# Global average pooling over rows of 8192: loads of 8 MB and 16 MB in turn, and rows summed as two halves

## The chip, the core and the metric

The kernel runs on one core of a Trainium2 chip. The time is that of one execution on the device in microseconds (us); each kernel has the median of several runs. The profile shows one further execution, whose length is its span, from the first instruction to the last.

The engines that matter are VectorE (DVE in the profile) and ScalarE (ACT), which do the sums, SyncE (SP), which only waits and issues transfers, and the 16 DMA engines, which bring the data from HBM into SBUF. TensorE is not used, and GpSimd (POOL) sets four constants at the start.

## The reference

```
x: (64, 256, 8192) float32
reference(x) = mean of x over its last axis      # (64, 256) float32
```

These are 16384 rows of 8192 numbers, 536.87 MB, read once; 65.5 KB are written. Each number takes part in one addition.

## The kernel before, in words

**How the rows are laid out.** The 16384 rows are seen as one long list. Each of the 128 partitions has 128 rows, in two parts: `own`, R = 111 rows that follow each other in memory, and `own2`, R2 = 17 rows from the end of the list. With L = 8192, a row is 32 KB on a partition. One row of `own` (its first) and one of `own2` (its last) are kept for the end; the other 126 rows per partition come in pairs, 63 loads of [128, 2L], 8 MB each.

**The buffers.** There are three, `bufs[0]` to `bufs[2]`, of 64 KB per partition each. Each has a semaphore that tells that its load has landed (`in_sems`) and one that counts how often it was read out (`free_sems`).

**SyncE** issues every transfer, in the order in which they stand (lines 97 to 129). The first load is cut into 1 MB and 7 MB (line 99), loads two and three follow at once (line 103). Then a loop (line 109) and a written-out rest (line 116) go around the buffers: wait until VectorE and ScalarE have both read the buffer, then issue its next load. After the last pair comes the tail: one row per partition, 4 MB, into the first half of `bufs[0]` (line 120), and the other one in six pieces of falling size (line 123), five into the second half of `bufs[0]` and the last into `fin`. At the end SyncE waits for VectorE twice and stores the results of `own` and `own2` (lines 125 and 127).

**VectorE** waits for a load and sums the first row of the pair into a column of `res` (line 136, a reduction). **ScalarE** waits for the same load, scales the second row by 1/L in place, and its accumulator gives the mean, written straight to the output tile `outsb` (line 174). So each load is read by both at the same time, and its buffer is free when the slower one is done.

**The tail.** VectorE first scales all of its sums into `outsb` (line 148). Then it takes 15/32 of the 4 MB row (line 156) while ScalarE takes the rest (line 186), and `total` (line 142) adds the two parts and scales. The pieces of the last row are split in the same way (lines 161 and 189). The last piece, in `fin`, has the partial sums beside it, and one more `total` adds and scales it all. Its store ends the kernel.

Of the kernel before, what the change touches and what calls it, by code (L numbers as in the profile page):

```python
# [6 lines left out]
ADD = mybir.AluOpType.add  # L7
MULT = mybir.AluOpType.mult
X = mybir.AxisListType.X
COPY = mybir.ActivationFunctionType.Copy  # L10


def bass_global_avg_pool_1d_kernel(
    nc: bass.Bass,
    x: bass.AP,
    out: bass.AP,
):
    P = 128
    B, C, L = x.shape
    rows = B * C  # L20
    assert rows % (2 * P) == 0 and L % 64 == 0
    inv = 1.0 / float(L)

    R2 = 17
    R = rows // P - R2
    assert R % 2 == 1 and R2 % 2 == 1
    NBUF = 3  # L30
    N1, N2 = R // 2, R2 // 2
    NFULL = N1 + N2
    NLOOP = NFULL // NBUF
    NLOAD = N1 // NBUF
    assert NLOOP * NBUF == NFULL and NLOAD >= 2
    M = P * R

    flat = x.rearrange("b c l -> (b c) l")
    own = flat[0:M, :].rearrange("(p r) l -> p (r l)", p=P)
    own2 = flat[M:rows, :].rearrange("(p r) l -> p (r l)", p=P)  # L40
    out_flat = out.rearrange("b c -> (b c)")
    out_own = out_flat[0:M].rearrange("(p r) -> p r", p=P)
    out_own2 = out_flat[M:rows].rearrange("(p r) -> p r", p=P)

    ch = [L // 2, 17 * L // 64, 7 * L // 64, L // 16, 3 * L // 128, 5 * L // 128]
    dve = [53 * L // 256, 13 * L // 128, 17 * L // 256, 5 * L // 256, 3 * L // 128]
    assert sum(ch) == L
    NCH = len(ch)  # L50
    NS = NCH - 2
    offs = [sum(ch[:c]) for c in range(NCH)]
    NPART = 2 * NS + 1

    with ExitStack() as ctx:
        sb = lambda n, s: ctx.enter_context(nc.sbuf_tensor(n, s, F32))
        sem = lambda n: ctx.enter_context(nc.semaphore(n))

        sb("pad0", [P, 32])

        fin = sb("fin", [P, 384])
        scaled = sb("scaled", [P, 384])
        half = sb("half", [P, 32])
        scaled_half = sb("scaled_half", [P, 32])
        res = sb("res", [P, 64])
        outsb = sb("outsb", [P, R + R2])
        sb("pad1", [P, 960])
        bufs = [sb(f"buf{i}", [P, 2 * L]) for i in range(NBUF)]

        in_sems = [sem(f"in_sem{i}") for i in range(NBUF)]  # L70
        free_sems = [sem(f"free_sem{i}") for i in range(NBUF)]
        tile_sem = sem("tile_sem")
        ch_sems = [sem(f"ch_sem{i}") for i in range(NCH)]
        act_sem = sem("act_sem")
        dve_sem = sem("dve_sem")
        out_sems = [sem(f"out_sem{i}") for i in range(2)]

        tail = bufs[0]
        D = 15 * L // 32

        def chunk(c):
            if c == NCH - 1:
                return fin[:, 0 : ch[c]]
            return tail[:, L + offs[c] : L + offs[c] + ch[c]]

        part = lambda i: fin[:, ch[-1] + i : ch[-1] + i + 1]

        D_HALF, D_TILE = 2, 3  # L90
        D_PART = D_TILE + NS + 1
        D_LAST = D_PART + 1

        A_HALF, A_PART = 1, 1 + NS


        eng = nc.sync
        for a, w in ((0, L // 4), (L // 4, 2 * L - L // 4)):
            eng.dma_start(bufs[0][:, a : a + w], own[:, L + a : L + a + w]).then_inc(  # L99
                in_sems[0], 16  # L100
            )
        for b in range(1, NBUF):
            eng.dma_start(bufs[b][:], own[:, (2 * b + 1) * L : (2 * b + 3) * L]).then_inc(
                in_sems[b], 16
            )
        with eng.Fori(1, NLOAD) as i:
            for b in range(NBUF):
                eng.wait_ge(free_sems[b], i * 2)
                eng.dma_start(  # L109
                    bufs[b][:], own[:, bass.ds((i * NBUF + b) * (2 * L) + L, 2 * L)]  # L110
                ).then_inc(in_sems[b], 16)
        for g in range(NLOAD * NBUF, NFULL):
            b = g % NBUF
            eng.wait_ge(free_sems[b], g // NBUF * 2)
            of, a = (own, 2 * g + 1) if g < N1 else (own2, 2 * (g - N1))
            eng.dma_start(bufs[b][:], of[:, a * L : (a + 2) * L]).then_inc(
                in_sems[b], 16
            )
        eng.wait_ge(free_sems[0], 2 * NLOOP)
        eng.dma_start(tail[:, 0:L], own[:, 0:L]).then_inc(tile_sem, 16)  # L120
        for c in range(NCH):
            a = (R2 - 1) * L + offs[c]
            eng.dma_start(chunk(c), own2[:, a : a + ch[c]]).then_inc(ch_sems[c], 16)  # L123
        eng.wait_ge(dve_sem, D_TILE)
        eng.dma_start(out_own, outsb[:, 0:R]).then_inc(out_sems[0], 16)
        eng.wait_ge(dve_sem, D_LAST)
        eng.dma_start(out_own2, outsb[:, R : R + R2]).then_inc(out_sems[1], 16)
        for s in out_sems:
            eng.wait_ge(s, 16)


        eng = nc.vector
        with eng.Fori(0, NLOOP) as i:
            for b in range(NBUF):
                eng.wait_ge(in_sems[b], i * 16 + (16 if b else 32))
                eng.tensor_reduce(  # L136
                    res[:, bass.ds(i * NBUF + b, 1)], bufs[b][:, 0:L], X, ADD
                ).then_inc(free_sems[b], 1)

        def total(to, junk, ap, after):  # L140
            eng.wait_ge(dve_sem, after)  # L141
            eng.tensor_scalar(  # L142
                junk, ap, inv, None, MULT, ADD, accum_out=to
            ).then_inc(dve_sem, 1)

        for b in range(NBUF):
            eng.wait_ge(free_sems[b], 2 * NLOOP)
        eng.tensor_scalar(  # L148
            outsb[:, 1 : 1 + 2 * NFULL].rearrange("p (n j) -> p j n", j=2)[:, 0],
            res[:, 0:NFULL],  # L150
            inv,
            None,
            MULT,
        ).then_inc(dve_sem, 1)
        eng.wait_ge(tile_sem, 16)
        eng.tensor_reduce(half[:, 0:1], tail[:, 0:D], X, ADD).then_inc(dve_sem, 1)  # L156
        eng.wait_ge(act_sem, A_HALF)
        total(outsb[:, 0:1], scaled_half[:, 0:2], half[:, 0:2], D_HALF)
        for c in range(NS + 1):
            eng.wait_ge(ch_sems[c], 16)  # L160
            eng.tensor_reduce(part(c), chunk(c)[:, 0 : dve[c]], X, ADD).then_inc(dve_sem, 1)  # L161
        eng.wait_ge(act_sem, A_PART)
        eng.wait_ge(ch_sems[NCH - 1], 16)
        w = ch[-1] + NPART
        total(outsb[:, 2 * NFULL + 1 : 2 * NFULL + 2], scaled[:, 0:w], fin[:, 0:w], D_PART)


        eng = nc.scalar
        eng.preload_act_table(COPY)  # L169
        with eng.Fori(0, NLOOP) as i:  # L170
            for b in range(NBUF):
                eng.wait_ge(in_sems[b], i * 16 + (16 if b else 32))
                ap = bufs[b][:, L : 2 * L]
                eng.activation(  # L174
                    ap,
                    ap,
                    COPY,
                    scale=inv,
                    accum_out=outsb[:, bass.ds((i * NBUF + b) * 2 + 2, 1)],
                ).then_inc(free_sems[b], 1)  # L180

        def summed(ap, to):
            eng.activation(ap, ap, COPY, accum_out=to).then_inc(act_sem, 1)  # L183

        eng.wait_ge(tile_sem, 16)
        summed(tail[:, D:L], half[:, 1:2])
        for c in range(NS):
            eng.wait_ge(ch_sems[c], 16)
            summed(chunk(c)[:, dve[c] :], part(NS + 1 + c))
# [28 lines left out]
```

## Time and profile before

| what | us |
|---|---|
| median of 3 runs (lowest, highest) | 1243.44 (1243.22, 1243.46) |
| span of the profiled execution | 1242.2 |
| VectorE busy | 556.4 |
| ScalarE busy | 458.6 |
| VectorE's waits for loads, before line 136 | 682.1 |
| ScalarE's waits for loads, before line 174 | 777.0 |
| SyncE's waits for VectorE at line 109, 51 of them | 964.1 |
| from issue to landing of an 8 MB load | 49.0 |

For the profiled execution the profile gives the span; the 1.2 us between it and the median lie outside its first and last instruction. A busy time is the sum of the engine's instructions; what is left of the span is waiting. A row of the groups gives line, engine, operation, output and input with their shapes, the count, then busy time and mean duration in ns, then the idle time just ahead of these instructions and what ended it. A row of the timeline starts with the start and the duration, both in us. A row of the chain is a step of the work that ended last, with start and duration; "SPq" and "DVEq" there are the engines' own waiting and issuing. "Landing" is the moment at which a transfer's semaphore says that all of it is there.

### The profile page before, as it was taken

Reading aid. Unit: us, or ns where it says so; the run is one execution under the profiler, and the core shown is the slowest. Engines: PE = TensorE matmul, PEld = TensorE weight load, DVE = VectorE, ACT = ScalarE, POOL = GpSimd, SP = SyncE. Lnnn points to the kernel's source line nnn. Section 1 sums busy time; section 2 is a strip of 40 time slices with the busy share of each in tenths; the row PEclk is TensorE's granted clock in tenths of the full one; section 3 lists DMA queues with packets and bytes.
Section 4 is the critical chain, followed back from the end, with each engine's and each line's share of the span. In section 5 each row is a group of like instructions: output and inputs, shape, how many; then the busy total and the mean of one; then the engine's idle time right before and its main releaser. Section 6 shows DMA issues by size and latency. Waiting matters only on the chain.

```text
span 1242.2 us, 756 instructions
## 1 busy us (share of the span) xinstructions
DVE 556.4 (45%) x74; ACT 458.6 (37%) x137; POOL 0.2 (0%) x4
## 2 busy tenths in 40 slices
DVE  2354353543534435345353453544535435354355
ACT  2243242442423424334243342433424324244245
POOL 0000000000000000000000000000000000000000
DMA  9999999999999999999999999999999999999998
GB/s 405 439 439 439 439 437 412 435 439 439 439 439 435 409 439 439 439 439 439 437 409 437 439 439 439 439 437 409 437 439 439 439 439 439 418 426 439 439 439 374
DMA packets 10512, 536.94 MB, mean 432 GB/s; under 512 B 1424, under 2 KB 1680, under 8 KB 1936
## 3 DMA queue, kind: packets, MB, share of 16 engines
q1 hardware_dynamic: 10512, 536.94, 99.8%
HBM read 536.87 MB, written 0.07 MB: 432 GB/s over the span
## 4 chain that ended last, share of the span: by engine, by line
DMA 84%; DVE 15%; SPq 0%; issue 0%; DVEq 0%
DMA buf<-in_x_dram 81%; DVE res L136 15%; DMA fin<-in_x_dram 4%; SPq L123 0%; SPq L109 0%; DVEq L136 0%; DVE scaled L142 0%; SPq L99 0%; SPq L120 0%; DVEq L141 0%
## 5 line engine op out<-in xcount | busy, mean ns | idle before, releaser
L136 DVE TENSOR_REDUCE res<-buf 128x8192 f32 x63 | 547.2, 8686 | 682.1 <-DMA buf<-in_x_dram 682.1
L174 ACT ACTIVATE buf<-buf 128x8192 f32<-128x8192 f32 x63 | 442.9, 7030 | 777.0 <-DMA buf<-in_x_dram 777.0
L174 ACT ACTIVATION_READ_ACCUMULATOR buf<-buf x63 | 11.7, 186 | 0.0
L183 ACT ACTIVATE buf<-buf 128x352 f32<-128x352 f32 (+3 forms) x5 | 8.3, 1663 | 3.6 <-DMA buf<-in_x_dram 3.6
L161 DVE TENSOR_REDUCE fin<-buf 128x1 f32<-128x1696 f32 (+4 forms) x5 | 4.2, 866 | 1.2 <-DMA buf<-in_x_dram 1.0
L156 DVE TENSOR_REDUCE half<-buf 128x1 f32<-128x3840 f32 x1 | 4.2, 4153 | 0.6 <-DMA buf<-in_x_dram 0.6
L169 ACT ACT_TABLE_LOAD x1 | 1.3, 1283 | 0.7 <-PEq L203 0.7
L183 ACT ACTIVATION_READ_ACCUMULATOR buf<-buf 128x1 f32 x5 | 0.9, 186 | 0.0
L142 DVE TENSOR_SCALAR_CACHE_REDUCE scaled<-fin 128x329 f32<-128x329 f32 x1 | 0.5, 497 | 0.2 <-DMA fin<-in_x_dram 0.2
L148 DVE TENSOR_SCALAR outsb<-res 128x63 f32<-128x63 f32 x1 | 0.2, 196 | 0.1
L142 DVE TENSOR_SCALAR_CACHE_REDUCE scaled_half<-half 128x2 f32<-128x2 f32 x1 | 0.2, 155 | 0.1
L203 POOL MEMSET const-bfloat16-1.0<- 128x1 bf16 x1 | 0.1, 101 | 0.0
L203 POOL MEMSET const-uint8-127<- 128x1 uint8 x1 | 0.1, 101 | 0.0
L203 POOL MEMSET const-float32-0.0<- 128x1 f32 x1 | 0.1, 98 | 0.2 <-issue 0.2
L203 POOL MEMSET const-float32-1.0<- 128x1 f32 x1 | 0.1, 98 | 0.0
L142 DVE DVE_READ_ACCUMULATOR scaled_half<-half 128x1 f32 x1 | 0.1, 83 | 0.0
L142 DVE DVE_READ_ACCUMULATOR scaled<-fin 128x1 f32 x1 | 0.1, 83 | 0.0
## 6 DMA issues: line engine op xcount, KB each, us to landing
buf<-in_x_dram SPq DMA_DIRECT2D x1, 7168.0 KB, 21.2
buf<-in_x_dram SPq DMA_DIRECT2D x1, 4096.0 KB, 39.5
buf<-in_x_dram SPq DMA_DIRECT2D x1, 2048.0 KB, 44.0
buf<-in_x_dram SPq DMA_DIRECT2D x1, 1088.0 KB, 46.1
buf<-in_x_dram SPq DMA_DIRECT2D x1, 1024.0 KB, 4.8
buf<-in_x_dram SPq DMA_DIRECT2D x62, 49.0
buf<-in_x_dram SPq DMA_DIRECT2D x1, 448.0 KB, 46.8
buf<-in_x_dram SPq DMA_DIRECT2D x1, 256.0 KB, 46.9
```

The source lines that it names most:

```text
L136: eng.tensor_reduce(res[:, bass.ds(i * NBUF + b, 1)], bufs[b][:, 0:L], X, ADD).then_inc(free_sems[b], 1)
L142: eng.tensor_scalar(junk, ap, inv, None, MULT, ADD, accum_out=to).then_inc(dve_sem, 1)
L148: eng.tensor_scalar(outsb[:, 1 : 1 + 2 * NFULL].rearrange("p (n j) -> p j n", j=2)[:, 0], res[:, 0:NFULL], inv, None, MULT,).then_inc(dve_ ...
L156: eng.tensor_reduce(half[:, 0:1], tail[:, 0:D], X, ADD).then_inc(dve_sem, 1)
L161: eng.tensor_reduce(part(c), chunk(c)[:, 0 : dve[c]], X, ADD).then_inc(dve_sem, 1)
L169: eng.preload_act_table(COPY)
L174: eng.activation(ap, ap, COPY, scale=inv, accum_out=outsb[:, bass.ds((i * NBUF + b) * 2 + 2, 1)],).then_inc(free_sems[b], 1)
L183: eng.activation(ap, ap, COPY, accum_out=to).then_inc(act_sem, 1)
L203: nc = _bacc.Bacc("TRN2", target_bir_lowering=False, num_devices=1)
```

## The change

- R2 goes from 17 to 19, and R from 111 to 109, so that both parts less one row are multiples of six.
- Three buffers of 64 KB per partition become two: `short` of 64 KB and `long` of 128 KB. A round loads two rows into `short` (8 MB) and the next four into `long` (16 MB). There are 21 rounds, 18 in `own` and 3 in `own2`: 42 loads in place of 63. SyncE waits for `short`, issues its load, waits for `long`, issues its load.
- In a round VectorE takes one row of `short` and three of `long`, ScalarE one of each.
- VectorE sums a row by a `scalar_tensor_tensor` of its two halves: the first half times 1.0 plus the second half, written over the first half, with the sum of the results in an accumulator. Before it was a reduction of the whole row.
- Before the tail VectorE scales its sums by two instructions, 21 x 1 and 21 x 3 columns, in place of one of 63 columns. They no longer count on `dve_sem`; the reduction of the half row counts two instead.
- The tail row and its pieces go to `short`. Their sizes, their split and their order stay.

```diff
-    R2 = 17
+    R2 = 19
     R = rows // P - R2
...
+    ROUND = 6
...
+    N1, N2 = (R - 1) // ROUND, (R2 - 1) // ROUND
+    NLOOP = N1 + N2
...
-        bufs = [sb(f"buf{i}", [P, 2 * L]) for i in range(NBUF)]
...
+        short = sb("short", [P, 2 * L])
+        long = sb("long", [P, 4 * L])
...
-        tail = bufs[0]
+        tail = short
...
+            eng.dma_start(short[:, a : a + w], own[:, L + a : L + a + w]).then_inc(in_s, 16)
+        eng.dma_start(long[:], own[:, 3 * L : 7 * L]).then_inc(in_l, 16)
+        with eng.Fori(1, N1) as i:
+            eng.wait_ge(free_s, i * 2)
+            eng.dma_start(short[:], own[:, bass.ds(i * (ROUND * L) + L, 2 * L)]).then_inc(in_s, 16)
+            eng.wait_ge(free_l, i * 4)
+            eng.dma_start(long[:], own[:, bass.ds(i * (ROUND * L) + 3 * L, 4 * L)]).then_inc(in_l, 16)
+        for g in range(N2):
...
+        eng.wait_ge(free_s, 2 * NLOOP)
         eng.dma_start(tail[:, 0:L], own[:, 0:L]).then_inc(tile_sem, 16)
...
+        def row(buf, r, to, free):
+            a = buf[:, r * L : r * L + L // 2]
+            b = buf[:, r * L + L // 2 : (r + 1) * L]
+            eng.scalar_tensor_tensor(a, a, 1.0, b, MULT, ADD, accum_out=to).then_inc(free, 1)
+
         with eng.Fori(0, NLOOP) as i:
-            for b in range(NBUF):
-                eng.wait_ge(in_sems[b], i * 16 + (16 if b else 32))
-                eng.tensor_reduce(
-                    res[:, bass.ds(i * NBUF + b, 1)], bufs[b][:, 0:L], X, ADD
-                ).then_inc(free_sems[b], 1)
+            eng.wait_ge(in_s, i * 16 + 32)
+            row(short, 0, res[:, bass.ds(i * 4, 1)], free_s)
+            eng.wait_ge(in_l, i * 16 + 16)
+            for r in range(3):
+                row(long, r, res[:, bass.ds(i * 4 + 1 + r, 1)], free_l)
...
+        eng.wait_ge(free_s, 2 * NLOOP)
+        eng.wait_ge(free_l, 4 * NLOOP)
+        rounds = outsb[:, 1 : 1 + ROUND * NLOOP].rearrange("p (n j) -> p n j", j=ROUND)
+        for to, of in ((0, 0), (2, 1)):
+            w = 3 if of else 1
+            eng.tensor_scalar(
...
         eng.wait_ge(tile_sem, 16)
-        eng.tensor_reduce(half[:, 0:1], tail[:, 0:D], X, ADD).then_inc(dve_sem, 1)
+        eng.tensor_reduce(half[:, 0:1], tail[:, 0:D], X, ADD).then_inc(dve_sem, 2)
...
+        def scaled_row(buf, r, to, free):
+            ap = buf[:, r * L : (r + 1) * L]
+            eng.activation(ap, ap, COPY, scale=inv, accum_out=to).then_inc(free, 1)
+
         with eng.Fori(0, NLOOP) as i:
...
+            eng.wait_ge(in_s, i * 16 + 32)
+            scaled_row(short, 1, outsb[:, bass.ds(i * ROUND + 2, 1)], free_s)
+            eng.wait_ge(in_l, i * 16 + 16)
+            scaled_row(long, 3, outsb[:, bass.ds(i * ROUND + 6, 1)], free_l)
```

More of the change, by code (lines that the diff above doesn't have):

```diff
@@ L22, in bass_global_avg_pool_1d_kernel @@
     inv = 1.0 / float(L)
-    R2 = 17
+    R2 = 19
     R = rows // P - R2
[L29 to L35, printed above, removed]
+    ROUND = 6
+    assert (R - 1) % ROUND == 0 and (R2 - 1) % ROUND == 0
+    N1, N2 = (R - 1) // ROUND, (R2 - 1) // ROUND
+    NLOOP = N1 + N2
     M = P * R
@@ L132, in bass_global_avg_pool_1d_kernel @@
         eng = nc.vector
+        def row(buf, r, to, free):
+            a = buf[:, r * L : r * L + L // 2]
+            b = buf[:, r * L + L // 2 : (r + 1) * L]
+            eng.scalar_tensor_tensor(a, a, 1.0, b, MULT, ADD, accum_out=to).then_inc(free, 1)
         with eng.Fori(0, NLOOP) as i:
-            for b in range(NBUF):
-                eng.wait_ge(in_sems[b], i * 16 + (16 if b else 32))
-                eng.tensor_reduce(
-                    res[:, bass.ds(i * NBUF + b, 1)], bufs[b][:, 0:L], X, ADD
-                ).then_inc(free_sems[b], 1)
+            eng.wait_ge(in_s, i * 16 + 32)
[3 more added lines that the diff above has]
+                row(long, r, res[:, bass.ds(i * 4 + 1 + r, 1)], free_l)
         def total(to, junk, ap, after):
@@ L144, in total @@
             ).then_inc(dve_sem, 1)
[L146 to L154, printed above, removed]
+        eng.wait_ge(free_s, 2 * NLOOP)
[4 more added lines that the diff above has]
+            eng.tensor_scalar(
+                rounds[:, :, to : to + w],
+                res[:, 0 : 4 * NLOOP].rearrange("p (n j) -> p n j", j=4)[:, :, of : of + w],
+                inv,
+                None,
+                MULT,
+            )
         eng.wait_ge(tile_sem, 16)
-        eng.tensor_reduce(half[:, 0:1], tail[:, 0:D], X, ADD).then_inc(dve_sem, 1)
+        eng.tensor_reduce(half[:, 0:1], tail[:, 0:D], X, ADD).then_inc(dve_sem, 2)
         eng.wait_ge(act_sem, A_HALF)
@@ L164, in bass_global_avg_pool_1d_kernel @@
         w = ch[-1] + NPART
-        total(outsb[:, 2 * NFULL + 1 : 2 * NFULL + 2], scaled[:, 0:w], fin[:, 0:w], D_PART)
+        total(outsb[:, R + R2 - 1 : R + R2], scaled[:, 0:w], fin[:, 0:w], D_PART)
         eng = nc.scalar
         eng.preload_act_table(COPY)
+        def scaled_row(buf, r, to, free):
+            ap = buf[:, r * L : (r + 1) * L]
+            eng.activation(ap, ap, COPY, scale=inv, accum_out=to).then_inc(free, 1)
         with eng.Fori(0, NLOOP) as i:
[L171 to L180, printed above, removed]
+            eng.wait_ge(in_s, i * 16 + 32)
+            scaled_row(short, 1, outsb[:, bass.ds(i * ROUND + 2, 1)], free_s)
+            eng.wait_ge(in_l, i * 16 + 16)
+            scaled_row(long, 3, outsb[:, bass.ds(i * ROUND + 6, 1)], free_l)
         def summed(ap, to):
```

33 lines of the change are left out of this document (9 added, 24 removed).

## The prediction

> **What bounds the kernel now.** I read the page first: the span, the 40 slices, the queues, the chain of work that ended last, the costliest groups.
>
> ```profile
> span 1242.2 us, 756 instructions
> ...
> DVE 556.4 (45%) x74; ACT 458.6 (37%) x137; POOL 0.2 (0%) x4
> ...
> GB/s 405 439 439 439 439 437 412 435 439 439 439 439 435 409 439 439 439 439 439 437 409 437 439 439 439 439 437 409 437 439 439 439 439 439 418 426 439 439 439 374
> DMA packets 10512, 536.94 MB, mean 432 GB/s; under 512 B 1424, under 2 KB 1680, under 8 KB 1936
> ...
> q1 hardware_dynamic: 10512, 536.94, 99.8%
> ...
> L136 DVE TENSOR_REDUCE res<-buf 128x8192 f32 x63 | 547.2, 8686 | 682.1 <-DMA buf<-in_x_dram 682.1
> L174 ACT ACTIVATE buf<-buf 128x8192 f32<-128x8192 f32 x63 | 442.9, 7030 | 777.0 <-DMA buf<-in_x_dram 777.0
> L174 ACT ACTIVATION_READ_ACCUMULATOR buf<-buf x63 | 11.7, 186 | 0.0
> ```
>
> The queue's packets fill 99.8% of the 16 DMA engines, while VectorE and ScalarE are idle for more than half the span and both wait for loads alone. So the stream of 536.94 MB sets the time, and faster arithmetic in the middle is worth nothing. Next the windows: the stretch between the first 8 MB landing and the last one, and the stretch in which the last 8 MB come in small pieces.
>
> ```profile
> 22.37:1220.47 1198.10, 538.53 (x62) 441.61 (x124) 0.00 (x0) 1.00 1.00 434
> 1220.47:1239.98 19.51, 17.38 (x10) 15.71 (x12) 0.00 (x0) 1.00 0.96 406
> ```
>
> The columns are length, VectorE, ScalarE and GpSimd busy, clock, DMA share, GB/s. In the stream the DMA share is 1.00. Whatever the change wins must come from outside VectorE and ScalarE there. What can still move is the end, and for it I read the timeline of VectorE.
>
> ```profile
> 22.52 8.69 DVE L136 TENSOR_REDUCE res<-buf 128x8192 f32 x1 [22.52 <-DMA buf<-in_x_dram]
> ...
> 1220.60 8.69 DVE L136 TENSOR_REDUCE res<-buf 128x8192 f32 x1 [10.68 <-DMA buf<-in_x_dram]
> 1229.42 0.20 DVE L148 TENSOR_SCALAR outsb<-res 128x63 f32<-128x63 f32 x1
> 1230.17 4.15 DVE L156 TENSOR_REDUCE half<-buf 128x1 f32<-128x3840 f32 x1 [0.55 <-DMA buf<-in_x_dram]
> 1234.46 0.15 DVE L142 TENSOR_SCALAR_CACHE_REDUCE scaled_half<-half 128x2 f32<-128x2 f32 x1
> 1234.55 0.08 DVE L142 DVE_READ_ACCUMULATOR scaled_half<-half 128x1 f32 x1
> 1234.99 1.92 DVE L161 TENSOR_REDUCE fin<-buf 128x1 f32<-128x1696 f32 x1 [0.36 <-DMA buf<-in_x_dram]
> 1237.59 2.38 DVE L161 TENSOR_REDUCE fin<-buf 128x1 f32<-128x832 f32 x4 [0.68 <-DMA buf<-in_x_dram]
> 1240.12 0.50 DVE L142 TENSOR_SCALAR_CACHE_REDUCE scaled<-fin 128x329 f32<-128x329 f32 x1 [0.15 <-DMA fin<-in_x_dram]
> 1240.54 0.08 DVE L142 DVE_READ_ACCUMULATOR scaled<-fin 128x1 f32 x1
> ```
>
> From the last big load on, VectorE waits four times for the next landing: 0.55, 0.36, 0.68 and 0.15 us. The first three, 1.59 us, are all the slack that it has behind the stream; work added there beyond 1.59 us moves the end.
>
> The median of the runs is 1243.44 us, 1.2 us above the profiled span; I add differences to the median.
>
> **The change part by part.**
>
> *63 loads become 42.* Row 1220.60 less row 22.52, over the 62 loads between, is 19.32 us per 8 MB load. What a load's boundary costs shows where the same bytes come in seven loads. The chain of waits gives the two landings:
>
> ```profile
> 22.52 8.70 DVE res L136
> 31.21 0.02 issue
> 31.23 0.07 SPq L109
> ...
> 31.40 49.00 DMA buf<-in_x_dram
> ...
> 1181.79 0.03 issue
> 1181.82 0.06 DVEq L136
> 1181.87 0.05 issue
> 1181.92 8.70 DVE res L136
> ...
> 1193.38 46.61 DMA fin<-in_x_dram
> 1239.98 0.02 issue
> ...
> 1240.12 0.50 DVE scaled L142 x2
> ```
>
> A landing stands 0.13 us ahead of the instruction that it releases (1181.79 to 1181.92). So the last big load landed at 1220.47, and the seven small ones were in at 1239.98: 19.51 us, 0.19 more than one load. Six further boundaries at 0.03 us each; 21 boundaries fewer are worth at most 21 x 0.03 = 0.7 us. The small loads also had seven packets where one load has one: the page's 10512 packets over 73 transfers (63 big loads, one of them in two parts; 7 small ones; 2 stores) are 144 each, 128 rows and 16 more. A 16 MB load has rows of 128 KB, and no row of that length is in this trace. If it is cut into two packets, only 16 packets per load go: per engine one in nine of what a small load brought, 0.03 / 9 x 21, under 0.1 us. If a row stays one packet, nearly all of the 0.7. I take 0.1, since no packet longer than today's 64 KB rows is seen, and keep 0.7 for the range. The Trainium skill (SBUF — State Buffer, section "The DMA setup-cost knee") puts some 2 us of fixed cost on every transfer, beside bytes over 436 GB/s; that is weighed as a rival below.
>
> *Two buffers for three.* Today a load is issued 49 us ahead of its landing. The DMA engines go empty if the long buffer comes free too late behind its landing: then only an 8 MB load, 19.32 us, stands between. The path is three VectorE rows, 13.28 us (next part), 0.13 us from landing to start, 0.19 us from the end of VectorE's work to SyncE's issue (31.21 to 31.40), and the way from issue to first bytes, bounded by the smallest loads:
>
> ```profile
> buf<-in_x_dram SPq DMA_DIRECT2D x1, 1024.0 KB, 4.8
> buf<-in_x_dram SPq DMA_DIRECT2D x62, 49.0
> ...
> out_dram<-outsb SPq DMA_DIRECT2D x1, 8.5 KB, 1.5
> ```
>
> 1.05 MB at 434 GB/s need 2.4 of the 4.8 us, so 2.4 us at most, and 1.5 us for the store. The sum is 16.0 us, and 3.3 us are left: no gap, cost nothing. The cover is gone once a row takes over (19.32 - 2.72) / 3 = 5.53 us. ScalarE needs 7.2 us on either buffer and comes before that. The short buffer is free 7.5 us after its landing, with 38.6 us of the long load ahead. SyncE waits in turn for the short buffer, then the long one; the long one's release always lies behind the short issue, so nothing queues wrongly. The start is untouched: the same 1 MB and 7 MB come first.
>
> *A row as two halves added.* It streams 4096 elements of two sources. Two reductions give the rate of VectorE:
>
> ```profile
> L156 DVE TENSOR_REDUCE half<-buf 128x1 f32<-128x3840 f32 x1 | 4.2, 4153 | 0.6 <-DMA buf<-in_x_dram 0.6
> L142 DVE TENSOR_SCALAR_CACHE_REDUCE scaled<-fin 128x329 f32<-128x329 f32 x1 | 0.5, 497 | 0.2 <-DMA fin<-in_x_dram 0.2
> ```
>
> (8686 - 4153) / (8192 - 3840) = 1.042 ns per element and 153 ns fixed; the accumulating form fits too (329 x 1.042 + 153 = 496 ns). Its accumulator read ends where the instruction itself ends (1240.54 + 0.08 and 1240.12 + 0.50), so it adds 0.01 us. If one pair passes per step, a row takes 4096 x 1.042 + 153 = 4.42, with the read 4.43 us. The ends, as no two-source form is in this trace: 2.29 us if two pairs pass per step, 8.69 us if the sources are taken one after the other. I take 4.43, nearest to the accumulating row, which takes one output per step. The Trainium skill (VectorE: DVE Perf Modes, "The perf-mode tier table" and the errata section) states one result per cycle for fp32 with two SBUF sources, (N + 151) / 0.96 ns; an estimate by it is 4.42 us, and the sum would be the same. In the stream VectorE's share falls (84 x 4.43 for 63 x 8.69) and ScalarE's too (42 rows for 63), hidden by the loads on both sides.
>
> *The last 16 MB load.* This is the term that counts. Behind the last big landing VectorE has three rows, not one: 13.28 us for 8.69. The tile of line 156 is there 9.57 us after the first row's start (1220.60 to 1230.17), so VectorE now comes late to it and to all chunks. From the first row's start: rows 13.28; wait for its own semaphore 0.13 (1229.29 to 1229.42); two scalings in place of one, at most 0.20 and at least 0.15 each, 0.36; half tile 4.15; 0.14 and 0.17 for its total; chunks 1.92 and 2.38, now without a wait; 0.15 and 0.50 for the last total. Sum 23.18 us. Before it is 20.02 (1220.60 to 1240.62): **+3.16 us**. Cross-check: 4.59 more in rows, 0.16 more in scalings, less 1.59 of slack, is 3.16. ScalarE has one row as today and is not late. The first store then goes out at 18.3 and is done before the second; the second lands as long after VectorE as today.
>
> Sum: +3.16 - 0.1 = +3.06, so 1243.44 + 3.06 = **1246.5 us** (span 1245.3). 0.2% of the time, 2.5 us, is what a measurement of this kernel can tell from no change; the forecast lies a little above it.
>
> **The rivals.**
>
> *A boundary between loads costs more than the end showed (not slower).* The best slices move 439 GB/s, at which 8.39 MB take 19.11 us: 0.21 us below the spacing. If all of that were the boundary, 21 fewer give 4.4 us back: 1242.1 us, no change by the bound. It decides for faster from (3.16 + 2.5) / 21 = 0.27 us per boundary. Against it: the slow slices (405 to 418) and the fast ones average out at the 434 of the long window, where the DMA share is 1.00. By the skill's 2 us the sum would be 1243.44 - 42 + 3.16 = 1204.6 us; the trace disagrees, since that rule makes one load 21.2 us and the spacing is 19.32, loads being queued behind each other.
>
> *VectorE's row is faster than one pair per step.* Below (9.57 - 0.49) / 3 = 3.03 us per row, the rows and scalings end before the tile lands, and the end is the stream's again: 1243.3 us, no change.
>
> *The long buffer comes free too late (much slower).* Above 5.53 us a row, the DMA engines idle in each of the 20 rounds that reissue the long load. At 8.69 us: 3 x 8.69 + 2.72 - 19.32 = 9.5 us each, 189 us in all, and 3 x 4.26 = 12.8 at the end: 1448 us. Against it is the accumulating row's one element per step.
>
> **How the numbers follow.** The forecast's mechanism has 0.82. Its low end is 0.7 for the packets and rows without their fixed 153 ns, 0.5: 1245.4. Its high end is a second fixed 0.15 and a separate 0.19 for the read, as ScalarE's 186 ns, on each row, 1.0, and the runs' spread of 0.24: 1247.8. Of it 0.12 lies below +2.5 us, which counts as the same. Boundaries 0.08, of it 0.02 faster. Faster rows 0.06. Late buffer 0.04. So faster 0.02, same 0.12 + 0.06 + 0.06 = 0.24, slower 0.70 + 0.04 = 0.74. The range goes down to the second rival: 1243.2 to 1247.8.
>
> **What would show it.** Right: in the stream a DMA share of 1.00 and 434 GB/s; SyncE's waits for the long buffer ending some 5 to 6 us ahead of the short landing; VectorE rows of 4.4 us; in the tail no waits ahead of lines 156 and 161 and the last total some 22.7 us behind the first of the last three rows; 10176 packets (10512 less 21 x 16), or 7488 if a long row is one packet. Wrong: rows far from 4.4 us, a DMA share below 1.00 with gaps of a fixed period of 58 us, or a landing of the last load earlier by over 1 us.

## The result and the profile after

| | before | after |
|---|---|---|
| median (lowest, highest), us | 1243.44 (1243.22, 1243.89) | 1245.81 (1245.65, 1245.96) |
| span of the profiled execution, us | 1242.2 | 1244.5 |

Both medians are over 17 runs. The ratio is 1.0018, with a 95% interval of 1.0012 to 1.0025: 2.4 us slower, clear of zero. The median lies just inside the 0.2% (2.5 us) that the prediction called no change; the interval, 1.5 to 3.1 us, has that bound within it. It forecast 1246.5, with a range of 1243.2 to 1247.8.

The page of the kernel after, with the lines that answer to those shown of before:

```profile
span 1244.5 us, 783 instructions
...
DVE 377.6 (30%) x180; ACT 309.0 (25%) x95; POOL 0.2 (0%) x4
...
DMA packets 10176, 536.94 MB, mean 431 GB/s; under 512 B 1088, under 2 KB 1344, under 8 KB 1600
...
q1 hardware_dynamic: 10176, 536.94, 99.6%
...
L128 DVE SCALAR_TENSOR_TENSOR long<-long 128x4096 f32<-128x4096 f32 x63 | 275.4, 4422 | 718.2 <-DMA long<-in_x_dram 718.2
...
L128 DVE SCALAR_TENSOR_TENSOR short<-short 128x4096 f32<-128x4096 f32 x21 | 92.9, 4425 | 146.9 <-DMA short<-in_x_dram 146.9
```

VectorE has lost 179 us of work and ScalarE 150, and the kernel is slower all the same, because neither was the limit. A row as two halves takes 4422 ns. The 10176 packets are those of long rows cut in two. The windows of the kernel after, first landing to last big landing and the rest of the stream (length, VectorE, ScalarE, GpSimd, clock, DMA share, GB/s):

```profile
22.62:1220.48 1197.86, 355.58 (x162) 292.04 (x82) 0.00 (x0) 1.00 1.00 434
1220.48:1240.07 19.59, 19.20 (x12) 15.72 (x12) 0.00 (x0) 1.00 0.96 404
```

The stream is the same: 434 GB/s at a share of 1.00. The last big landing is at 1220.48 us, before it was 1220.47, and the last piece lands at 1240.07, before 1239.98. So the difference lies behind the last big landing. The timeline of VectorE there (start, duration, instruction):

```profile
1220.62 4.42 DVE L128 SCALAR_TENSOR_TENSOR long<-long 128x4096 f32<-128x4096 f32 x1 [34.21 <-DMA long<-in_x_dram]
1224.97 0.08 DVE L128 DVE_READ_ACCUMULATOR long<-long  x1
1224.97 4.42 DVE L128 SCALAR_TENSOR_TENSOR long<-long 128x4096 f32<-128x4096 f32 x1
1229.31 0.08 DVE L128 DVE_READ_ACCUMULATOR long<-long  x1
1229.31 4.42 DVE L128 SCALAR_TENSOR_TENSOR long<-long 128x4096 f32<-128x4096 f32 x1
1233.66 0.08 DVE L128 DVE_READ_ACCUMULATOR long<-long  x1
1233.85 0.29 DVE L148 TENSOR_SCALAR outsb<-res 128x21 f32<-128x21 f32 x2
1234.05 4.14 DVE L156 TENSOR_REDUCE half<-short 128x1 f32<-128x3840 f32 x1
1238.33 0.15 DVE L139 TENSOR_SCALAR_CACHE_REDUCE scaled_half<-half 128x2 f32<-128x2 f32 x1
1238.41 0.08 DVE L139 DVE_READ_ACCUMULATOR scaled_half<-half 128x1 f32 x1
1238.41 3.96 DVE L161 TENSOR_REDUCE fin<-short 128x1 f32<-128x1696 f32 x5
1242.53 0.50 DVE L139 TENSOR_SCALAR_CACHE_REDUCE scaled<-fin 128x329 f32<-128x329 f32 x1 [0.15 <-DVE fin L161]
1242.95 0.08 DVE L139 DVE_READ_ACCUMULATOR scaled<-fin 128x1 f32 x1
```

Behind the first row no instruction waits for a landing any more: the brackets with a DMA that stood at lines 156 and 161 before are gone, and the last `total` waits for VectorE itself where it waited for the last piece. From the first row's start to the last total's start VectorE needs 21.91 us (1220.62 to 1242.53); before it was 19.52 (1220.60 to 1240.12). The difference, 2.39 us, is the whole loss of 2.37 us between the medians. An instruction that follows another without a wait starts some 0.08 us before the recorded end of the one ahead: rows of 4.42 us start 4.35 us apart.

### The profile page after: what moved, and what is told of

It reads as the page before. It is cut to its first block, busy times and chain, and to the rows that moved or that the text cites. A ratio compares the mean times of both kernels' runs of the same rounds, so it can differ in the third digit from the quotient of the medians.

```text
span 1244.5 us, 783 instructions
## 1 busy us (share of the span) xinstructions
DVE 377.6 (30%) x180; ACT 309.0 (25%) x95; POOL 0.2 (0%) x4
## 2 busy tenths in 40 slices
DMA packets 10176, 536.94 MB, mean 431 GB/s; under 512 B 1088, under 2 KB 1344, under 8 KB 1600
## 3 DMA queue, kind: packets, MB, share of 16 engines
q1 hardware_dynamic: 10176, 536.94, 99.6%
## 4 chain that ended last, share of the span: by engine, by line
DMA 73%; DVE 16%; issue 7%; another core or an unknown queue 3%; DVEq 0%; SPq 0%
DMA long<-in_x_dram 72%; DVE long L128 15%; DMA short<-in_x_dram 2%; DVE half L156 0%; DVE fin L161 0%; DVEq L130 0%; DVEq L128 0%; SPq L103 0%; DVE scaled L139 0%; SPq L97 0%; DVE outsb L148 0%; DVE short L128 0%; DVE scaled_half L139 0%; DVEq L138 0%
## 5 line engine op out<-in xcount | busy, mean ns | idle before, releaser
L128 DVE SCALAR_TENSOR_TENSOR long<-long 128x4096 f32<-128x4096 f32 x63 | 275.4, 4422 | 718.2 <-DMA long<-in_x_dram 718.2
L173 ACT ACTIVATE long<-long 128x8192 f32<-128x8192 f32 x21 | 147.6, 7030 | 661.6 <-DMA long<-in_x_dram 661.6
L173 ACT ACTIVATE short<-short 128x8192 f32<-128x8192 f32 x21 | 147.6, 7030 | 264.9 <-DMA short<-in_x_dram 264.9
L128 DVE SCALAR_TENSOR_TENSOR short<-short 128x4096 f32<-128x4096 f32 x21 | 92.9, 4425 | 146.9 <-DMA short<-in_x_dram 146.9
L182 ACT ACTIVATE short<-short 128x352 f32<-128x352 f32 (+3 forms) x5 | 8.3, 1665 | 3.7 <-DMA short<-in_x_dram 3.7
L128 DVE DVE_READ_ACCUMULATOR long<-long x63 | 5.2, 82 | 0.0
L156 DVE TENSOR_REDUCE half<-short 128x1 f32<-128x3840 f32 x1 | 4.1, 4142 | 0.0
L161 DVE TENSOR_REDUCE fin<-short 128x1 f32<-128x1696 f32 (+4 forms) x5 | 4.0, 858 | 0.0
L173 ACT ACTIVATION_READ_ACCUMULATOR long<-long x21 | 3.9, 186 | 0.0
L173 ACT ACTIVATION_READ_ACCUMULATOR short<-short x21 | 3.9, 186 | 0.0
## 6 DMA issues: line engine op xcount, KB each, us to landing
short<-in_x_dram SPq DMA_DIRECT2D x1, 4096.0 KB, 41.1
```

The costliest lines, as they stand in the source:

```text
L128: eng.scalar_tensor_tensor(a, a, 1.0, b, MULT, ADD, accum_out=to).then_inc(free, 1)
L173: eng.activation(ap, ap, COPY, scale=inv, accum_out=to).then_inc(free, 1)
```

## The experiments

In the diffs "..." stands for lines that are not shown.

**An 8 MB load at the end.** The round is turned round: the long load first, the short one last, and the tail goes to the long buffer. Loads, buffers and halves stay.

```diff
-        tail = short
+        tail = long
...
         with eng.Fori(1, N1) as i:
+            eng.wait_ge(free_l, i * 4)
+            eng.dma_start(long[:], own[:, bass.ds(i * (ROUND * L) + L, 4 * L)]).then_inc(in_l, 16)
             eng.wait_ge(free_s, i * 2)
+            eng.dma_start(short[:], own[:, bass.ds(i * (ROUND * L) + 5 * L, 2 * L)]).then_inc(in_s, 16)
...
+            eng.wait_ge(in_l, i * 16 + 32)
+            for r in range(3):
+                row(long, r, res[:, bass.ds(i * 4 + r, 1)], free_l)
+            eng.wait_ge(in_s, i * 16 + 16)
+            row(short, 0, res[:, bass.ds(i * 4 + 3, 1)], free_s)
...
```

> The rounds, the two buffers, the 42 loads and the rows as halves stay; only the order in a round is turned round, so that an 8 MB load is the last one ahead of the tail (the tail goes to the long buffer). Theory (the 2.4 us are VectorE's three rows behind the last 16 MB load): VectorE has one row of 4.4 us there, is done with its scalings about 5 us after that landing and waits for the tile at about 9.6 us as in the kernel before: 1243.4 us, within 0.4. Rival A (42 longer loads on two buffers slow the stream): nothing in the stream changes, so 1245.8 us. Rival B (a row as two halves costs time in the stream or at the end): also 1245.8 us.

Measured: 1243.47 us (11 runs) beside 1243.48 for the kernel before, ratio 0.9999 (0.9990 to 1.0008). Its timeline of VectorE at the end:

```profile
1220.71 4.43 DVE L128 SCALAR_TENSOR_TENSOR short<-short 128x4096 f32<-128x4096 f32 x1 [6.20 <-DMA short<-in_x_dram]
...
1227.86 0.29 DVE L148 TENSOR_SCALAR outsb<-res 128x63 f32<-128x63 f32 x2 [2.71 <-ACT short L173]
1230.40 4.15 DVE L156 TENSOR_REDUCE half<-long 128x1 f32<-128x3840 f32 x1 [2.26 <-DMA long<-in_x_dram]
...
1240.31 0.50 DVE L139 TENSOR_SCALAR_CACHE_REDUCE scaled<-fin 128x329 f32<-128x329 f32 x1 [0.15 <-DVE fin L161]
```

The wait for the tile is back, and with it the time of before, though every other part of the change is still in. The long loads, the two buffers and the halves together cost nothing that can be measured (the interval is about 1 us to either side); the place of the long load costs 2.4 us.

**The halves alone**, in the kernel before.

```diff
-                eng.tensor_reduce(
-                    res[:, bass.ds(i * NBUF + b, 1)], bufs[b][:, 0:L], X, ADD
-                ).then_inc(free_sems[b], 1)
+                u, v = bufs[b][:, 0 : L // 2], bufs[b][:, L // 2 : L]
+                eng.scalar_tensor_tensor(
+                    u, u, 1.0, v, MULT, ADD, accum_out=res[:, bass.ds(i * NBUF + b, 1)]
+                ).then_inc(free_sems[b], 1)
```

> The kernel before with one part of the change alone: VectorE sums its row as two halves, on the three buffers and the 63 loads. Theory: VectorE gets 4.3 us faster per row, everywhere under the loads and in the tail too, where it then waits longer for the tile: 1243.4 us, no change, and the wait ahead of the tile's reduction grows from 0.55 to about 4.8 us. Rival B (the two-source form slows the transfers that write SBUF beside it): up to 2.4 us more, 1245.8 us. A fourth kind of result, faster by more than 0.5 us, would say that VectorE's pace counts in the stream.

Measured: 1243.65 us (11 runs), ratio 1.0002 (0.9993 to 1.0011): no change. Its timeline of VectorE behind the last big landing:

```profile
1221.12 4.43 DVE L137 SCALAR_TENSOR_TENSOR buf<-buf 128x4096 f32<-128x4096 f32 x1 [14.93 <-DMA buf<-in_x_dram]
...
1228.38 0.20 DVE L149 TENSOR_SCALAR outsb<-res 128x63 f32<-128x63 f32 x1 [2.83 <-ACT buf L175]
1230.69 4.15 DVE L157 TENSOR_REDUCE half<-buf 128x1 f32<-128x3840 f32 x1 [2.10 <-DMA buf<-in_x_dram]
```

The time that a faster row frees turns into waiting: 2.83 us for ScalarE's row and 2.10 for the tile, 4.9 together, where the kernel before waits 0.55. Expected were 4.8 us ahead of the tile alone: I had left out that the scaling waits for ScalarE's last row too.

**One more piece of work at the end.** In the last round alone, VectorE first reduces half a row into a column that nothing reads.

```diff
-        with eng.Fori(0, NLOOP) as i:
+        with eng.Fori(0, NLOOP - 1) as i:
...
+        i = NLOOP - 1
...
+        eng.wait_ge(in_l, i * 16 + 16)
+        eng.tensor_reduce(res[:, 96:97], long[:, L // 2 : L], X, ADD)
+        for r in range(3):
...
```

> The kernel after, and in the last round alone VectorE does one more reduction of half a row (4096 elements, 4.42 us, into a column that nothing reads) ahead of its three rows of the long buffer. Theory: VectorE is the chain from the last big landing to the end, so all of it is added: 1245.8 + 4.4 = 1250.2 us, within 0.3. Rival A (the stream sets the end): 1245.8 us, or less than 2 us more.

Measured: 1250.0 us (4 runs), ratio to before 1.0052 (1.0036 to 1.0067), 4.2 us above the kernel after. Timeline of VectorE:

```profile
1220.69 4.42 DVE L140 TENSOR_REDUCE res<-long 128x1 f32<-128x4096 f32 x1 [34.20 <-DMA long<-in_x_dram]
1225.03 4.41 DVE L128 SCALAR_TENSOR_TENSOR long<-long 128x4096 f32<-128x4096 f32 x1
...
1246.93 0.50 DVE L146 TENSOR_SCALAR_CACHE_REDUCE scaled<-fin 128x329 f32<-128x329 f32 x1 [0.15 <-DVE fin L168]
```

The piece takes 4.34 us from start to start (1220.69 to 1225.03), and the last total moves from 21.91 to 26.24 us behind the first start. All of it reaches the end: VectorE is the chain there.

**Whole-row reductions on two buffers.** This prices the rival in which the long buffer comes free too late.

```diff
-            a = buf[:, r * L : r * L + L // 2]
-            b = buf[:, r * L + L // 2 : (r + 1) * L]
-            eng.scalar_tensor_tensor(a, a, 1.0, b, MULT, ADD, accum_out=to).then_inc(free, 1)
+            eng.tensor_reduce(to, buf[:, r * L : (r + 1) * L], X, ADD).then_inc(free, 1)
```

> The kernel after with VectorE's rows summed by the reduction of the whole row, 8.69 us each. It puts the price of the long buffer coming free too late to the test. Theory: from the long landing 0.13 to the start, 26.06 for three rows, 0.19 to SyncE's issue and 1.5 to 2.4 us to the first bytes, against 19.32 us of the short load: the DMA engines idle 8.6 to 9.4 us in each of 20 rounds, 171 to 189 us; at the end 3 x 4.3 = 13 us more; together 1430 to 1448 us, rounds of 66.5 to 67.4 us in place of 58.0, and a DMA share of some 0.86. Rival (the queue holds enough work to cover it, or VectorE's pace in the stream counts for nothing): 1259 us, the 13 us at the end alone.

Measured: 1449.85 us (1 run), 2 us above the top of what was expected. Its page, and its timeline over one round:

```profile
span 1448.5 us, 699 instructions
...
q1 hardware_dynamic: 10176, 536.94, 86.5%
```

```profile
263.54 25.87 DVE L126 TENSOR_REDUCE res<-long 128x8192 f32 x3 [33.17 <-DMA long<-in_x_dram]
...
282.81 7.03 ACT L171 ACTIVATE short<-short 128x8192 f32<-128x8192 f32 x1 [12.15 <-DMA short<-in_x_dram]
...
289.58 0.38 SPq L103 DMA_DIRECT2D long<-in_x_dram  x1
...
330.84 7.03 ACT L171 ACTIVATE long<-long 128x8192 f32<-128x8192 f32 x1 [40.91 <-DMA long<-in_x_dram]
```

The long load is issued 6.9 us after the short one has landed (289.58, against 282.81 less 0.13), and a round takes 67.3 us here and 67.5 in the mean, 9.5 more than 58.0. The load lands 41.1 us after its issue; its bytes take 38.6. So the restart costs 2.5 us in this round, and 2.7 by the median of 41.3 us from issue to landing; I had called 2.4 an upper bound. The packet records of this round say where it goes: the sixteen packets that come first begin 1.0 to 1.8 us after the issue and take 2.7 to 3.2 us each, the sixteen behind them 2.42. In this kernel the halves are not idle arithmetic: without them the two buffers cost over 200 us.

**How late the long load may be issued.** In the kernel after SyncE issues it 5.9 us ahead of the short one's landing:

```profile
235.42 4.43 DVE L128 SCALAR_TENSOR_TENSOR long<-long 128x4096 f32<-128x4096 f32 x1 [34.23 <-DMA long<-in_x_dram]
...
248.71 0.38 SPq L103 DMA_DIRECT2D long<-in_x_dram  x1
...
254.70 4.43 DVE L128 SCALAR_TENSOR_TENSOR short<-short 128x4096 f32<-128x4096 f32 x1 [6.16 <-DMA short<-in_x_dram]
```

Three kernels shorten this lead by one more reduction in every round but the last, of 4096 elements, then of 2048 and 3072:

```diff
...
+            eng.tensor_reduce(res[:, bass.ds(i + 96, 1)], long[:, L // 2 : L], X, ADD)
             for r in range(3):
...
```

> The kernel after, and in every round but the last VectorE does one more reduction of half a row (4096 elements, 4.35 us from start to start, into a column that nothing reads) ahead of its three rows of the long buffer. It asks where the margin of the two buffers ends. Behind the long landing come 0.13 us, 17.5 us of VectorE and 0.2 us to SyncE's issue, 17.8 us, against 19.32 us of the short load: 1.5 us are left for the way to the first bytes. In the run with whole-row reductions the long load landed 41.4 us after its issue, 2.8 us above its 38.6 us of bytes, with idle stretches of 8.2 us. Theory A (while the short load still runs, only the way to the first packet counts, some 1.2 us, and it just fits): 1245.8 to 1247 us. Theory B (the whole 2.8 us are paid in every round): 1.2 to 1.3 us in each of 20 rounds, 1270 us.

Measured: 1301.79 us (4 runs, 1292.9 to 1304.8), ratio 1.0444 (1.0405 to 1.0484). Both theories missed. Timeline of one of its rounds:

```profile
240.60 4.42 DVE L134 TENSOR_REDUCE res<-long 128x4096 f32 x1 [36.89 <-DMA long<-in_x_dram]
...
258.22 0.38 SPq L103 DMA_DIRECT2D long<-in_x_dram  x1
...
260.09 4.42 DVE L128 SCALAR_TENSOR_TENSOR short<-short 128x4096 f32<-128x4096 f32 x1 [2.04 <-DMA short<-in_x_dram]
...
301.75 4.42 DVE L134 TENSOR_REDUCE res<-long 128x4096 f32 x1 [37.22 <-DMA long<-in_x_dram]
```

The issue comes 1.7 us ahead of the landing (260.09 less 0.13, less 258.22), and still the round takes 61.15 us (240.60 to 301.75), 3.2 more than 58.0. That asked for two points in between.

> As the run with a half row more in every round but the last, but with a reduction of 2048 elements, 2.2 us. That run missed both numbers (1301.8 us): SyncE issued the long load some 1.7 us ahead of the short one's landing and every round took 3.2 us more. Here the issue comes some 3.7 us ahead of the landing; in the kernel after it is 5.9. Theory C (an issue that is there before an engine starts its last packet, some 2.4 us ahead of the end, costs nothing; one that comes later leaves engines empty and costs some 3 us whatever is missing): 1245.8 us. Theory D (a fixed lead of 1.7 + 3.2 = 4.9 us is needed and what is missing is paid): 1.2 us in each of 19 rounds, 1268 us.

> The same with a reduction of 3072 elements, 3.3 us: the long load is issued some 2.7 us ahead of the short one's landing. Theory C: 1245.8 us, or, if the way from issue to the engines' queues counts too, near the 1301 us of 1.7 us of lead. Theory D: 2.2 us in each of 19 rounds, 1288 us.

Measured: 1259.55 us (4 runs; ratio 1.0125, 1.0108 to 1.0142) and 1274.89 us (4 runs; 1.0250, 1.0233 to 1.0268). The lead in the fourth round of the kernel with 2048 elements more is 3.7 us (254.73 less 0.13, less 250.93):

```profile
250.93 0.38 SPq L103 DMA_DIRECT2D long<-in_x_dram  x1
...
254.73 4.43 DVE L128 SCALAR_TENSOR_TENSOR short<-short 128x4096 f32<-128x4096 f32 x1 [3.97 <-DMA short<-in_x_dram]
```

The leads of the table are read in the same way.

| lead, us | time, us | over the kernel after, per round (20) |
|---|---|---|
| 5.9 (the kernel after) | 1245.81 | 0 |
| 3.7 | 1259.55 | 0.7 |
| 2.7 | 1274.89 | 1.5 |
| 1.7 | 1301.79 | 2.8 |
| -6.9 (whole-row reductions) | 1449.85 | 9.6, less the end |

The last row: 204 us more, of them 12.8 at the end (its last total starts 34.67 us behind its first row, not 21.91), 191 in 20 rounds. Theory C, free or a fixed price, falls: the price rises with what is missing. Theory D, a fixed lead of 4.9 us, has the direction right, but is too dear at 3.7 and 2.7 us (1268 and 1288 expected). What it lacks shows in the rounds of the kernel with 3.7 us of lead; the starts of its added reduction, one a round, from the timeline of VectorE:

```profile
61.23 2.29 DVE L134 TENSOR_REDUCE res<-long 128x2048 f32 x1 [34.18 <-DMA long<-in_x_dram]
...
293.36 2.29 DVE L134 TENSOR_REDUCE res<-long 128x2048 f32 x1 [34.19 <-DMA long<-in_x_dram]
...
351.98 2.29 DVE L134 TENSOR_REDUCE res<-long 128x2048 f32 x1 [34.82 <-DMA long<-in_x_dram]
...
470.12 2.29 DVE L134 TENSOR_REDUCE res<-long 128x2048 f32 x1 [35.46 <-DMA long<-in_x_dram]
...
529.82 2.29 DVE L134 TENSOR_REDUCE res<-long 128x2048 f32 x1 [35.96 <-DMA long<-in_x_dram]
```

The first four rounds take 58.03 us each (61.23 to 293.36), as in the kernel after; the ninth start comes 59.7 us after the eighth (470.12 to 529.82). The same lead is free at first and dear later. The semaphore events of the trace say what changed with it: each landing is sixteen increments, as many as there are DMA engines. From the first to the last of the sixteen it is 0.3 to 0.5 us in those first rounds, and 1.1 to 3.3 us from the sixth long landing on; in the kernel after it closes from 0.66 to 0.4 us and stays there.

One reading fits, though no run isolates it: with a short lead the engines fall out of step, a landing waits for the last of them, and engines that were done earlier stand empty until the next issue. Empty engines are not the whole price. The page of this kernel has

```profile
q1 hardware_dynamic: 10176, 536.94, 99.1%
```

so its packets took 99.1% of 1261.3 us, 1250 us, and those of the kernel after 99.6% of 1244.5 us, 1240 us. Of the 16.8 us more in these two spans, some 10 are packets that took longer and some 6 are empty engines. What first puts the engines out of step was not looked into. With less lead the first reissue already costs: the first two added reductions start 59.4 us apart at 2.7 us of lead (61.14 and 120.50) and 58.9 us apart at 1.7 us (61.22 and 120.15), not 58.0.

**Twice as many loads.** The kernel before, with each 8 MB load but the first issued as two of 4 MB, a row each.

```diff
...
-                eng.dma_start(
-                    bufs[b][:], own[:, bass.ds((i * NBUF + b) * (2 * L) + L, 2 * L)]
-                ).then_inc(in_sems[b], 16)
+                for h in range(2):
+                    eng.dma_start(
+                        bufs[b][:, h * L : (h + 1) * L],
+                        own[:, bass.ds((i * NBUF + b) * (2 * L) + (1 + h) * L, L)],
+                    ).then_inc(in_sems[b], 16)
...
```

> The kernel before with each 8 MB load but the first issued as two of 4 MB, a row each: 62 boundaries more. It measures the price of a boundary by itself. Theory (0.03 us per boundary, from the seven small loads at the end of the kernel before): 2 us more, 1245.5 us. Rival (0.21 us, from the 439 GB/s of the best slices): 13 us more, 1256.5 us. By the Trainium skill's page on SBUF, some 2 us of fixed cost per transfer, it would be 124 us more, 1367 us.

Measured: 1246.08 us (10 runs) beside 1243.56, ratio 1.0020 (1.0010 to 1.0029). Its page:

```profile
DMA packets 19440, 536.95 MB, mean 431 GB/s; under 512 B 2416, under 2 KB 2672, under 8 KB 2928
...
q1 hardware_dynamic: 19440, 536.95, 100.0%
```

2.5 us for 62 boundaries is 0.04 us each, with 8928 packets more (62 x 144). The rows of these loads are half as long too, so 0.04 us is the boundary and the smaller packets together. The rival's 0.21 us is out. So are the 2 us that the Trainium skill (SBUF — State Buffer, "The DMA setup-cost knee") puts on a transfer, for loads that stand in line behind others; that a lone transfer pays such a price is not contradicted, since the restart above cost 2.5 to 2.7 us.

## Why the prediction was right

Direction, mechanism and place were right: 2.4 us slower where 3.06 was forecast, from VectorE's three rows behind the last 16 MB load. Moving that load away takes the loss back, and more work there adds its full length.

*The end, +3.16 us forecast, +2.39 measured.* This is the mis-sized term, 0.77 us too much. By parts, measured for forecast: rows with the wait to the scalings 13.23 (1220.62 to 1233.85) for 13.41; scalings 0.20 for 0.36; half tile with its wait 4.28 for 4.29; its total 0.08 for 0.17; chunks with the wait behind them 4.12 for 4.45. Most of it, over 0.5 us, is one slip: I added the recorded durations of instructions that follow each other, and they overlap by about 0.08 us. The trace of before had shown it: its accumulator read starts at 1234.55, before the end of the instruction ahead (1234.46 and 0.15). I used that for the read and not for the instruction behind it. The other 0.2 us is a wait that I took for work. The four reductions that stand there in 2.38 us have one in their midst that came late:

```profile
L161 DVE TENSOR_REDUCE fin<-buf 128x1 f32<-128x544 f32 x1 | 0.7, 720 | 0.1
```

It started 0.12 us after the one ahead had ended, as its piece had just landed, and not 0.08 us before. So the slack was more than the 1.59 us of the three waits that I counted.

By its own rule of 0.2%, the prediction gave 0.70 to slower beyond that bound and 0.12 to the same mechanism below it; the median came out there, 0.1 us below the bound. So the likelier side of the bound was missed, and by less than the measurement can tell.

*The row, 4.43 us* as one pair per step: 4422 ns recorded. An estimate by the formula that the Trainium skill gives for `tensor_tensor` in fp32 (VectorE: DVE Perf Modes, the section on the TRN2 errata) is 4.42 us as well; the trace agrees. The rival of faster rows is out.

*The loads, -0.1 us.* The packets fell to 10176, so long rows are cut in two and only 16 packets per load went. In the profiled executions the last big landing is 0.01 us later, not earlier: the first 8 MB landed 0.25 us later (22.62 for 22.37). The run with more work at the end, whose loads are the same, had that landing at 22.32, so this is scatter of the start. Between the two landings the stream took 0.24 us less (1197.86 for 1198.10), the way that was forecast, but no more than that scatter.

*Two buffers, nothing.* Right for this kernel: the issue came 5.9 us ahead, within the 5 to 6 forecast, and the DMA share stayed 1.00. The margin was too generous. I left 3.3 us and a threshold of 5.53 us a row; the runs show a price at 3.7 us of lead already, which is a threshold below 4.35 + 2.2 / 3 = 5.1 us a row. The 2.4 us for the way to the first bytes came from a load onto empty queues, as it should for that, but nothing in it shows engines out of step. That no rounds were lost rests on a lead that happened to be well above what is needed, not on a margin that had been worked out rightly.

*The price of the late buffer, 1448 us* at 8.69 us a row: 1449.85 measured, 9.6 us for the 9.5 a round and 12.8 for the 12.8 at the end.

*A faster kernel* did not come out of this. With the long load first the time is that of before: its first 16 MB are in at 41.8 us, where the kernel before has its first two loads in at 41.7, and the stream's 434 GB/s and some 2.2 us from the last landing to the end are the same in both. A smaller last piece could shorten its 0.50 us total; it was not tried, as the gain would be less than the spread of the runs.

## What to carry to other kernels

Where the transfers set the time, look at what stands behind the last big landing: the longer the last load, the more work falls due at once where no transfer hides it, so end on the short load and keep the long one ahead of it. For a chain of instructions without waits, sum the distances from start to start, not the recorded durations. With two buffers, leave the reissue a lead well beyond the time that a single transfer needs to get going; here 5.9 us was free in every round, and 3.7 us was free only at first.

## What the runs showed of the hardware that was not expected

A lead of 3.7 us was free while the sixteen increments of a landing lay 0.5 us apart, and cost about 1 us a round in the mean once they lay 2 to 3 us apart, within one execution. A late issue 1.7 us ahead of the landing cost more at restart than one 6.9 us behind it: the long load landed 43.5 us after its issue (median) in the one, of which 1.7 went to waiting for the short load, which leaves 41.8, and 41.3 us in the other, with 38.6 us of bytes in both. In the restart on empty queues that was read above, the first packets took 2.7 to 3.2 us, where those behind them took 2.42. A boundary between queued loads cost 0.04 us, smaller packets included.
